# A four-layer gMLP, pooling and ConvFFN trunk on eight cores: tile-wise stage borders and a scheduler that orders all instructions, in place of hand-placed order

## The chip, the cores and the metric

One Trainium2 chip, all eight cores. Every core does one prompt sequence (2048 tokens) and 64 sample tokens, without talking to the others, so the work is the same on all. The time is the device time of the slowest core, in microseconds (us).

Some executions of the kernels here fell in a second, slower state: the cores of one die, or of both, show a lower granted TensorE clock, and the run is some per cent longer. All comparisons below are between runs outside that state ("fast" runs).

## The reference

Four layers. Even layers mix tokens by spatial gating in chunks of 128, odd ones by trailing means over 2, 4, 8 and 16 tokens. A gated feed-forward stage with a causal convolution of width 3 follows each. There is an RMS norm before every part.

```python
D_MODEL = 1024; SEQ = 2048; DEPTH = 4; CHUNK = 128; D_V = 2048; D_FF = 2816
def rmsnorm(x, g):
    y = x * lax.rsqrt(jnp.mean(x * x, axis=-1, keepdims=True) + EPS)
    return y * g
def gmlp_mixer(h, w_in, g_v, w_s, b_s, w_out):
    z = jax.nn.gelu(jnp.einsum('btd,de->bte', h, w_in))
    u, v = jnp.split(z, 2, axis=-1)
    v = rmsnorm(v, g_v)
    s = jnp.einsum('hij,bcjhe->bcihe', tril(w_s), chunks(v)) + b_s    # (names shortened)
    return jnp.einsum('bte,ed->btd', u * s, w_out), v
def pool_mixer(h, buf, start_pos, w_pool, scale): ...  # (mean - h) @ w_pool per group, x scale
def conv_ffn(h, buf, w_gate, w_val, conv_w, conv_b, w_down):
    a, val = h @ w_gate, h @ w_val
    conv = conv_b + conv_w[0]*a[t-2] + conv_w[1]*a[t-1] + conv_w[2]*a[t]
    return (jax.nn.silu(conv) * val) @ w_down
# trunk: x = x + mixer(rmsnorm(x)); x = x + conv_ffn(rmsnorm(x)); last: rmsnorm(x)
```

## The kernel before

The residual x lies transposed on the chip: 1024 channels as eight rows of 128 partitions, tokens along the columns. Two groups of 1056 tokens (1024 of the prompt and 32 sample tokens) are computed one after the other, each in three tiles of 352 columns. Weights stream through a ring of four slots.

An instruction is issued at once, in the order in which the code calls it, on an engine and with PSUM banks that the code names:

```python
PE.op(mmg, reads=ug["res"] + hr, writes=[bank_r[gbk]])   # op() puts the waits in front and issues
ACC_BANKS = [3, 4]; SSQ_BANKS = [0, 1, 2]; gbanks = [0, 1, 2]; vbanks = [5, 6, 7]
```

The projections at the end of a stage go by weights first: for each of the eight output rows all three token tiles. So all three tiles are complete only at the very end, together, and the last statistics, root and norm stand behind them:

```python
    def chunk(self, dc, mm_emit, evac_emit, hooks=None):
        last = (dc == KC - 1)
        for tt in range(3):
            ...
            mm_emit(dc, tt, bk)
            if self.pend is not None and tt == 0:
                norm_mm(self.pend)                 # statistics of row dc-1, on TensorE
            evac_emit(dc, tt, bk)                  # x += psum, on VectorE
            if last:
                norm_square(dc, tt)
                if tt >= 1: norm_mm(dc, tt - 1); norm_rstd(tt - 1)
        if last:
            norm_mm(dc, 2); norm_rstd(2)
            if keep_warm: ...                      # off (0)
```

In a gating stage ScalarE has Gelu, then a root, then Gelu again for each chunk of 128 tokens, with a load of its function table each way (ACT_TABLE_LOAD, 68 in the gating stages, 1283 ns each):

```python
ACT.op(... out=junk, in_=vsb, func=AF.Square, accum_out=vstat[:, 0:1])
ACT.op(... out=vstat[:, 1:2], in_=vstat[:, 0:1], func=AF.Sqrt, bias=epsb, scale=1.0 / DV)
DVE.op(... reciprocal(out=vstat[:, 2:3], in_=vstat[:, 1:2]))
DVE.op(... scalar_tensor_tensor(out=vb, in0=vsb, scalar=vstat[:, 2:3], in1=gvb, op0=mult, op1=mult))
```

In the feed-forward stage the gate is copied to SBUF (`asb`) so that two earlier columns can be read across tile borders; the first tap comes from PSUM on ScalarE, the other two from the copy on VectorE. x is loaded by rows of tokens and transposed on TensorE (fp32, 128 tokens at a time), and y goes back the same way.

Of the kernel before, what the change touches and what calls it, by code (L numbers as in the profile page):

```python
# [7 lines left out]
BF16 = mybir.dt.bfloat16  # L8
AF = mybir.ActivationFunctionType
# [11 lines left out]
NS = 32  # L21
NT = NP + NS
TT = 352
# [4 lines left out]
SLOT = 4096  # L28
NSLOT = 4
# [14 lines left out]
class Tick:  # L44
    __slots__ = ("sem", "val", "clock")

    def __init__(self, sem, val, clock):
        self.sem, self.val, self.clock = sem, val, clock
# [5 lines left out]

class Eng:
    def __init__(self, name, handle, sem, self_safe=False):
        self.name, self.h, self.sem, self.self_safe = name, handle, sem, self_safe
        self.count = 0
        self.know = {}
        self.nwaits = 0  # L60
        self.nops = 0

    def _wait(self, t):
        key = t.sem.name
        if self.know.get(key, 0) >= t.val:
            return
        self.h.wait_ge(t.sem, t.val)
        self.nwaits += 1
        self.know[key] = t.val
        for k, v in t.clock.items():  # L70
            if self.know.get(k, 0) < v:
                self.know[k] = v

    def op(self, fn, reads=(), writes=(), dsem=None):
        best = {}

        def add(t, raw):
            k = t.sem.name
            if k not in best:
                best[k] = [t, raw]  # L80
            else:
                if best[k][0].val < t.val:
                    best[k][0] = t
                best[k][1] = best[k][1] or raw
        for r in reads:
            for o in r.overl:
                if o.last_write is not None:
                    add(o.last_write, True)
                if r.space == "ps":
                    for t in o.reads:  # L90
                        add(t, False)
        for w in writes:
            for o in w.overl:
                if o.last_write is not None:
                    add(o.last_write, False)
                for t in o.reads:
                    add(t, False)
        for t, raw in best.values():
            if t.sem is self.sem and (self.self_safe or not raw):
                continue  # L100
            self._wait(t)
        ins = fn(self.h)
        self.nops += 1
        if dsem is not None:
            dsem.count += 16
            ins.then_inc(dsem.sem, 16)
            tick = Tick(dsem.sem, dsem.count, dict(self.know))
        else:
            self.count += 1
            ins.then_inc(self.sem, 1)  # L110
            tick = Tick(self.sem, self.count, dict(self.know))
        for r in reads:
            r.reads.append(tick)
            if len(r.reads) > 48:
                b = {}
                for t in r.reads:
                    k = t.sem.name
                    if k not in b or b[k].val < t.val:
                        b[k] = t
                r.reads = list(b.values())  # L120
        for w in writes:
            w.last_write = tick
            w.reads = []
        return tick

def tiles_of(c0, c1):
    return list(range(c0 // TT, (c1 - 1) // TT + 1))

def build_program(cfg=None):
    cfg = cfg or {}  # L130
    nlayers = cfg.get("nlayers", DEPTH)
    do_mixer = cfg.get("do_mixer", True)
    do_ffn = cfg.get("do_ffn", True)
    ngroups = cfg.get("ngroups", NG)
    layers = cfg.get("layers", list(range(nlayers)))
    pool_dbg = cfg.get("pool_dbg", 99)
    keep_warm = cfg.get("keep_warm", 0)

    nc = bass.Bass("TRN2", target_bir_lowering=False)
    dr = {}  # L140

    def din(name, shape):
        dr[name] = nc.dram_tensor(name, list(shape), F32, kind="ExternalInput").ap()
        return dr[name]

    def dout(name, shape):
        dr[name] = nc.dram_tensor(name, list(shape), F32, kind="ExternalOutput").ap()
        return dr[name]

    x_prompt = din("x_prompt", [SEQ, D])  # L150
    x_sample = din("x_sample", [NSEQ * 4, D])
    state_pool = din("state_pool", [2, NSEQ * 15, D])
    state_ffn = din("state_ffn_conv", [DEPTH, NSEQ * 2, DFF])
    norm_mix = din("norm_mix", [DEPTH, D])
    norm_ffn = din("norm_ffn", [DEPTH, D])
    norm_final = din("norm_final", [1, D])
    w_in_a = din("w_in_a", [2, D, 2 * DV])
    g_v_a = din("g_v_a", [2, DV])
    w_s_a = din("w_s_a", [2, 8, 128, 128])
    b_s_a = din("b_s_a", [2, 8 * 128])  # L160
    w_out_a = din("w_out_a", [2, DV, D])
    w_pool_b = din("w_pool_b", [2, 1024, 256])
    scale_b = din("scale_b", [2, D])
    w_gate = din("w_gate", [DEPTH, D, DFF])
    w_val = din("w_val", [DEPTH, D, DFF])
    conv_w = din("conv_w", [DEPTH * 3, DFF])
    conv_b = din("conv_b", [DEPTH, DFF])
    w_down = din("w_down", [DEPTH, DFF, D])
    c_ident = din("c_ident", [128, 128])
    c_maskT = din("c_maskT", [128, 128])  # L170
    c_icnt = din("c_icnt", [128, 64])

    y_prompt = dout("y_prompt", [SEQ, D])
    y_sample = dout("y_sample", [NSEQ * 4, D])
    gmlp_v = dout("gmlp_v_sample", [2, NSEQ * 4, DV])
    pool_prompt = dout("pool_prompt", [2, 15, D])
    pool_sample = dout("pool_sample", [2, NSEQ * 15, D])
    conv_prompt = dout("ffn_conv_prompt", [DEPTH, 2, DFF])
    conv_sample = dout("ffn_conv_sample", [DEPTH, NSEQ * 2, DFF])

    es = ExitStack()
    with es:
        ARENA_BYTES = 212800
        arena = es.enter_context(nc.sbuf_tensor("arena", [128, ARENA_BYTES // 4], F32))
# [4 lines left out]
        def al(x):  # L189
            return (x + 31) // 32 * 32  # L190

        def esz(dt):
            return 4 if dt == F32 else 2
# [4 lines left out]
        def alloc_at(name, shape, dt, off):  # L198
            nb = int(np.prod(shape[1:])) * esz(dt)
            assert off + nb <= base + ARENA_BYTES, (name, off + nb - base, ARENA_BYTES)  # L200
            return nc.alloc_sbuf_tensor_at(name, list(shape), dt, offset=off), nb

        def alloc(name, shape, dt, off=None, pieces=None):
            b = Buf()
            if off is None:
                off = cursor[0]
                adv = True
            else:
                adv = False
            b.t, nb = alloc_at(name, shape, dt, off)  # L210
            b.off = off
            b.nb = nb
            if adv:
                cursor[0] = off + (nb + 31) // 32 * 32
            b.r = {}
            if pieces is None:
                b.r[None] = Res(reg, "sb", off, off + nb, name)
                b.all = [b.r[None]]
            else:
                for key, lo, hi in pieces:  # L220
                    b.r[key] = Res(reg, "sb", off + lo * esz(dt), off + hi * esz(dt), f"{name}{key}")
                b.all = list(b.r.values())
            return b

        def grid_pieces(nrow, rowlen, ncols=NT, coloff=0):
            ps = []
            for k in range(nrow):
                for tt in range(3):
                    ps.append(((k, tt), k * rowlen + coloff + tt * TT, k * rowlen + coloff + (tt + 1) * TT))
            return ps  # L230

        xT = alloc("xT", [128, KC, NT], F32, pieces=grid_pieces(KC, NT))
        ring = [alloc(f"ring{i}", [128, SLOT], BF16) for i in range(NSLOT)]
        ident = alloc("ident", [128, 128], F32)
        maskT = alloc("maskT", [128, 128], F32)
        icnt = alloc("icnt", [128, 4, 16], F32)
        onesb = alloc("onesb", [128, 128], BF16)
        epsb = alloc("epsb", [128, 1], F32)
        pvd = alloc("pvd", [128, KC, 12], F32)
        pvf = alloc("pvf", [128, FC, 16], F32)  # L240
        wsT = alloc("wsT", [128, 2, 8, 128], BF16)
        msm = alloc("msm", [32, 2, 8, 32], BF16)
        brow = alloc("brow", [1, 2, 8, 32], BF16)
        brow.all = [Res(reg, "virt", i, i + 1, f"brow{i}") for i in range(16)]
        browM = alloc("browM", [1, EC, 128], BF16)
        browM.all = [Res(reg, "virt", 50 + i, 51 + i, f"browM{i}") for i in range(2)]
        msm.all = [Res(reg, "virt", 100 + i, 101 + i, f"msm{i}") for i in range(16)]
# [105 lines left out]
        def evac_copy(out_ap, in_ap, reads, writes, eng=None):  # L353
            evac_flip[0] ^= 1
            if eng is not None:
                evac_flip[0] = eng
# [819 lines left out]
```

## Time and profile before

| | |
|---|---|
| median | 3419.86 us (16 runs, 3413.87 to 3906.85) |
| fast runs | 3412 to 3428 us |
| TensorE busy | 3019.6 us of a span of 3416.6 (88%) |
| mean granted clock | 0.943 to 0.947 |
| columns streamed through TensorE | 6,654,520 in 19,338 matmuls |

The prediction shows the lines of this profile. In them PE is TensorE (matmuls), PEld its weight loads, DVE is VectorE, ACT ScalarE, POOL GpSimd and SP SyncE; psum is PSUM, which every matmul row of the profiles writes, and the other names are tiles in SBUF. The clock is the share of TensorE's full clock that the records show as granted. A row of slices has 40 digits, each the busy tenths of one fortieth of the span. A group of instructions reads: line, engine, operation, out<-in, shapes, count | busy us, mean ns | idle time of the engine in front of them, with what ended most of it. A timeline row reads: start, length, line, shapes, count, and in brackets the idle time before it and what ended it.

### The profile page before, as it was taken

How to read it: one execution, taken by the hardware profiler on the slowest of the kernel's cores; microseconds unless marked ns; L12 is line 12 of the kernel's file. 1: busy time of each engine (PE TensorE's matmuls, PEld its weight loads, DVE VectorE, ACT ScalarE, POOL GpSimd, SP SyncE). 2: the span in 40 equal slices, each digit the busy share in tenths (PEclk: the TensorE clock that was granted, in tenths of full speed). 3: DMA queues.
4: the chain of work that ended last, by engine and by line, in shares of the span. 5: the costliest groups of instructions: out<-in, count | busy, mean ns of one | idle time of the engine just before them, and what ended most of it. 6: DMA issues, size and time to landing. Idle time of an engine off the chain costs nothing.

```text
span 3416.6 us, 52100 instructions; the slowest of 8 cores (3406.7 to 3416.6 us)
## 1 busy us (share of the span) xinstructions
PE 3019.6 (88%) x19338; PEld 1886.7 (55%) x19338; DVE 1639.2 (48%) x3353; ACT 1406.5 (41%) x2766; POOL 233.5 (7%) x245
## 2 busy tenths in 40 slices
PE   3888997699998999589969899968999989986997
PEld 2545665366554566356645456635665456653665
DVE  1143763675223573567341457456721437636753
ACT  2362542254254452345234536334523626522541
POOL 1000000001100001000100000100011000000010
PEclk9898998799999999799979999989999999998999
DMA  5713366156571347224857124732487233651463
GB/s 111 103 16 55 56 75 78 19 75 74 71 99 18 62 63 82 39 44 63 87 148 99 18 46 76 75 50 45 63 100 103 30 55 52 79 79 20 75 67 68
DMA packets 369235, 225.23 MB, mean 66 GB/s; under 512 B 189457, under 2 KB 362689, under 8 KB 368346
## 3 DMA queue, kind: packets, MB, share of 16 engines
q0 software_dynamic: 352320, 190.87, 43.6%
q1 hardware_dynamic: 16666, 31.03, 2.9%
q8 instruction: 157, 2.57, 0.3%
q14 instruction: 92, 0.75, 0.1%
HBM read 399.41 MB, written 13.32 MB: 121 GB/s over the span
## 4 chain that ended last, share of the span: by engine, by line
PE 72%; DVE 11%; ACT 8%; issue 5%; DMA 3%; SPq 0%; DVEq 0%; ACTq 0%
PE psum L1094 18%; PE psum L1002 17%; PE psum L996 17%; PE psum L783 7%; PE psum L693 7%; DVE hB L521 4%; DVE vn L725 2%; ACT vsb L714 2%; PE psum L502 2%; ACT junk L720 2%; PE psum L878 2%; DMA xstg<-x_prompt 1%; ACT sq L489 1%; DVE pA L930 1%; PE psum L708 1%
## 5 line engine op out<-in xcount | busy, mean ns | idle before, releaser
L996 PE MATMUL psum<-hB,ring 128*128 128x352 bf16 x4224 | 726.9, 316 | 36.8 <-DVE hB L521 34.6
L1002 PE MATMUL psum<-hB,ring 128*128 128x352 bf16 x4224 | 723.9, 315 | 8.9 <-DVE mT L1054 7.7
L1094 PE MATMUL psum<-mT,ring 128*128 128x352 bf16 x4224 | 643.0, 313 | 0.0
L996 PEld LDWEIGHTS psum<-hB,ring 128*128 128x128 bf16 x4224 | 415.4, 99 | 263.3 <-issue 41.8
L1002 PEld LDWEIGHTS psum<-hB,ring 128*128 128x128 bf16 x4224 | 414.0, 98 | 236.2 <-issue 17.1
L1094 PEld LDWEIGHTS psum<-mT,ring 128*128 128x128 bf16 x4224 | 412.7, 98 | 217.0 <-issue 1.3
L489 ACT ACTIVATE sq<-xT 128x1056 bf16<-128x1056 f32 x128 | 137.6, 1082 | 918.1 <-DVE xT L1100 520.4
L1016 ACT ACTIVATE asb<-psum 128x352 f32<-128x352 f32 x528 | 240.2, 455 | 532.9 <-PE psum L996 299.4
L1026 DVE SCALAR_TENSOR_TENSOR c2b<-asb,pvf,c0b 128x352 f32<-128x352 f32 x528 | 302.0, 572 | 241.1 <-ACT c0b L1022 239.0
L1100 DVE TENSOR_TENSOR xT<-psum,xT 128x352 f32<-128x352 f32 x192 | 100.8, 525 | 537.1 <-PE psum L1094 533.5
L1022 ACT ACTIVATE c0b<-psum,pvf 128x352 f32<-128x352 f32 x528 | 340.5, 645 | 0.0
L1029 DVE SCALAR_TENSOR_TENSOR c2b<-asb,pvf,c2b 128x352 f32<-128x352 f32 x528 | 302.7, 573 | 55.1
L1053 ACT ACTIVATE gb<-c2b 128x352 f32<-128x352 f32 x528 | 263.4, 499 | 35.6 <-DVE c2b L1029 18.4
L1054 DVE TENSOR_TENSOR mT<-gb,psum 128x352 bf16<-128x352 f32 x528 | 271.6, 514 | 9.5 <-ACT gb L1053 8.7
L693 PE MATMUL psum<-hB,ring 128*128 128x352 bf16 x1536 | 247.8, 326 | 29.2 <-DVE hB L521 29.2
L783 PE MATMUL psum<-UB,ring 128*128 128x352 bf16 x1536 | 253.1, 327 | 16.2 <-DVE UB L764 11.1
L708 PE MATMUL psum<-R,hB 128*128 128x512 bf16 (+1 forms) x1152 | 254.9, 380 | 9.3 <-ACT vsb L714 9.2
L693 PEld LDWEIGHTS psum<-hB,ring 128*128 128x128 bf16 x1536 | 154.6, 101 | 122.2 <-issue 35.2
L783 PEld LDWEIGHTS psum<-UB,ring 128*128 128x128 bf16 x1536 | 155.2, 102 | 105.3 <-issue 17.0
L708 PEld LDWEIGHTS psum<-R,hB 128*128 128x128 bf16 (+1 forms) x1152 | 111.0, 98 | 142.8 <-issue 14.4
L724 DVE RECIPROCAL vstat<-vstat 128x1 f32<-128x1 f32 (+1 forms) x36 | 5.8, 162 | 357.4 <-ACT vstat L722 357.4
L697 ACT ACTIVATE UB<-psum 128x352 bf16<-128x352 f32 x192 | 88.9, 463 | 158.0 <-PE psum L693 158.0
(114 smaller groups left out, 2162.7 us busy)
## 6 DMA issues: line engine op xcount, KB each, us to landing
ring<-w_down POOLq DMA_DIRECT2D x64, 704.0 KB, 8.9
ring<-w_gate POOLq DMA_DIRECT2D x40, 1024.0 KB, 9.7
ring<-w_val POOLq DMA_DIRECT2D x40, 1024.0 KB, 13.3
ring<-w_in_a POOLq DMA_DIRECT2D x16, 1024.0 KB, 9.9
ring<-w_out_a POOLq DMA_DIRECT2D x16, 1024.0 KB, 23.5
R<-w_in_a POOLq DMA_DIRECT2D x16, 1024.0 KB, 28.1
xstg<-x_prompt SPq DMA_DIRECT2D x16, 512.0 KB, 5.1
y_prompt<-stg SPq DMA_DIRECT2D x16, 512.0 KB, 3.2
```

Source lines behind the costliest of these rows:

```text
L693: i = e.matmul(bank(bk, 0, TT), lhsT=wv[:, kc, (ec % 4) * 128:(ec % 4 + 1) * 128], rhs=hB.t[:, kc, cs], start=(kc == 0), stop=(kc == KC - 1))
L708: i = e.matmul(psum[0:ntok, n * 512:(n + 1) * 512], lhsT=hB.t[:, kc, col0:col0 + ntok], rhs=R2.t[:, n, kc, :], start=(kc == 0), stop=(kc = ...
L783: i = e.matmul(bank(bk, 0, TT), lhsT=wv[:, ec, (dc % 2) * 128:(dc % 2 + 1) * 128], rhs=UB.t[:, ec, cs], start=(ec == 0), stop=(ec == EC - 1))
L996: ins = e.matmul(bank(gbk, 0, TT), lhsT=ug["view"][:, kc, fo:fo + 128], rhs=hB.t[:, kc, cs], start=(kc == 0), stop=(kc == KC - 1))
L1002: ins = e.matmul(bank(vbk, 0, TT), lhsT=uv["view"][:, kc, fo:fo + 128], rhs=hB.t[:, kc, cs], start=(kc == 0), stop=(kc == KC - 1))
L1016: ACT.op(lambda e: e.activation(out=ab.t[:, 2 + pc0:2 + pc0 + npr], in_=bank(gbk, 0, npr), func=AF.Copy), reads=[bank_r[gbk]], writes=abw)
L1022: ACT.op(lambda e: e.activation(out=cb.t[:, :], in_=bank(gbk, 0, TT), func=AF.Identity, bias=pvf.t[:, fc, 12 + l:13 + l], scale=pvf.t[:, f ...
L1026: DVE.op(lambda e: e.scalar_tensor_tensor(out=c2.t[:, 0:npr], in0=ab.t[:, 1 + pc0:1 + pc0 + npr], scalar=pvf.t[:, fc, 3 * l + 1:3 * l + 2] ...
L1029: DVE.op(lambda e: e.scalar_tensor_tensor(out=c2.t[:, 0:npr], in0=ab.t[:, pc0:pc0 + npr], scalar=pvf.t[:, fc, 3 * l:3 * l + 1], in1=c2.t[: ...
L1053: ACT.op(lambda e: e.activation(out=gg.t[:, :], in_=c2.t[:, :], func=AF.Silu), reads=c2.all, writes=gg.all)
L1054: DVE.op(lambda e: e.tensor_tensor(out=mT.t[:, fc, cs], in0=gg.t[:, :], in1=bank(vbk, 0, TT), op=ALU.mult), reads=gg.all + [bank_r[vbk]], ...
L1094: i = e.matmul(bank(bk, 0, TT), lhsT=wv[:, fc, :], rhs=mT.t[:, fc, cs], start=(fc == 0), stop=(fc == FC - 1))
```

## The change

The intent is to keep TensorE fed across the borders of stages. The network stays the same. Nearly the whole program is rewritten; the parts that bear on the time:

```diff
 # 1. record everything, then put it in order
-    def op(self, fn, reads=(), writes=(), dsem=None):    # issues at once
+class Recorder:
+    def rec(self, eng, fn, reads=(), writes=(), cost=0.0, dsem=None, nbytes=0, tab=None, pt=()): ...
+    def schedule(self, engines, window=160):
+        # list scheduler: of the next 160 recorded operations of each engine, the one that can
+        # start first by modelled costs; a PSUM tile gets the banks that come free first
 ...
 # 2. token tiles: sizes, sample tokens all in the first group
-TT = 352
+TILES = {0: [(0, 384), (384, 384), (768, 320)], 1: [(0, 384), (384, 384), (768, 256)]}
 ...
 # 3. projections go tile by tile; what follows a tile is recorded right behind it
+            for t in range(3):
+                proj_tile(g, t, mm_list)
+                after_tile(t)      # statistics, root, norm; pooling; store y and load the next x
 ...
 # 4. statistics: squares added on GpSimd, one matmul closes the sum
-                        norm_mm(self.pend)
+            eng = POOL if kc < KC - 1 else DVE
+            rec(eng, lambda e: e.tensor_tensor(out=d.t[:, 0:n], in0=a.t[:, 0:n], in1=s.t[:, 0:n], op=ALU.add), ...)
 ...
 # 5. reciprocal root of the gating norm: seven tiny VectorE operations, no table change
-                        ACT.op(lambda e: e.activation(... func=AF.Sqrt ...))
-                        DVE.op(lambda e: e.reciprocal(...))
+                rsqrt_col(vs, nt)
 ...
 # 6. feed-forward: no copy; the gate is computed with two more columns, all taps read PSUM
-                        ACT.op(lambda e: e.activation(out=ab.t[:, 2 + pc0:2 + pc0 + npr], in_=bank(gbk, 0, npr), func=AF.Copy), ...)
+                                i = e.matmul(pap(gb, 0, n + 2), lhsT=wg.t[:, kc, fs], rhs=hB.t[:, kc, c0:c0 + n + 2], ...)
 ...
 # 7. pooling: product with w_pool first, then a banded matrix, placed between the tiles around it
+                            lst.append(((oc, oc + 128), zt.t[:, zh, es_], band.t[:, gi, :], True))
+                            lst.append(((oc, oc + 16), zp.t[:, zh, es_], bprev.t[:, gi, :], False))
 ...
 # 8. the host packs x, weights and state as they lie on the chip
-                PE.op(trx, reads=[sres] + ident.all, writes=[bank_r[bk]])        # transposes of x and y
+        m["x_in"] = np.concatenate(parts)
```

## The prediction

> **What bounds the kernel now.** I read the cores first: spans of 3406.7 to 3416.6 us and clocks of 0.943 to 0.947, both dies alike, so the profile fell in an undisturbed run. Then the busy table and the slices, the windows of the slices, the timeline of TensorE at the start and in two stages, the waits, and the groups by form.
>
> From the page of the kernel before:
>
> ```profile
> span 3416.6 us, 52100 instructions; the slowest of 8 cores (3406.7 to 3416.6 us)
> PE 3019.6 (88%) x19338; PEld 1886.7 (55%) x19338; DVE 1639.2 (48%) x3353; ACT 1406.5 (41%) x2766; POOL 233.5 (7%) x245
> ...
> PE   3888997699998999589969899968999989986997
> ...
> PEclk9898998799999999799979999989999999998999
> ...
> PE 72%; DVE 11%; ACT 8%; issue 5%; DMA 3%; SPq 0%; DVEq 0%; ACTq 0%
> ```
>
> TensorE is the bound (88% busy, 72% of the chain that ended last), no other engine is half full, and where the PE row dips (5, 6, 7) the clock row dips too. The same seen in windows of one slice each (PE busy, PEld, DVE, ACT, POOL, clock, DMA share, GB/s):
>
> ```profile
> 0.00:85.00 85.00, 27.77 (x134) 19.86 (x134) 8.59 (x21) 17.38 (x24) 13.35 (x29) 0.92 0.59 111
> 598.00:683.00 85.00, 55.17 (x318) 32.97 (x319) 52.89 (x99) 21.96 (x40) 0.96 (x1) 0.78 0.11 19
> 683.00:769.00 86.00, 86.00 (x578) 56.15 (x577) 62.59 (x157) 50.55 (x120) 5.24 (x6) 1.00 0.50 74
> 1708.00:1793.00 85.00, 58.07 (x322) 38.51 (x321) 38.27 (x71) 31.49 (x48) 2.78 (x4) 0.76 0.56 149
> ```
>
> In the feed-forward stage (683 to 769) TensorE never stops, is granted the whole clock, and does a 352-column matmul every 86.00/578 = 149 ns: 352/2.4 = 146.7 plus about 2.4 ns. At the start, in the pooling layer (598 to 683) and between the two token groups (1708 to 1793) it stands still a third to two thirds of the time, and its clock falls. So I split the span: columns streamed, 6,654,520 (counted in the built program) / 2.4 per ns = 2773; 19338 matmuls x 2.4 ns = 46; the 288 fp32 transposes take 1.94 us per eight instead of 0.43, so about 50 more: 2870 us if warm and never waiting. Busy is 3020, so 150 us are the slow clock. Idle is 3417 - 3020 = 397 us. What can be had by keeping TensorE fed is therefore up to about 550 us, and the rest is columns.
>
> Where the idle time is, from the timeline of TensorE (start, length, line; idle before it in brackets) at the first layer and in a gating stage:
>
> ```profile
> 97.05 2.50 PE L693 MATMUL psum<-hB,ring 128*128 128x352 bf16 x8 [5.11 <-DVE hB L521]
> ...
> 1888.42 1.02 PE L742 MATMUL psum<-browM,onesb 1*128 1x512 bf16 x4 [0.33 <-DVE vn L725]
> 1889.38 1.07 PE L745 MATMUL psum<-wsT,vn 128*128 128x128 bf16 x16
> 1890.82 7.07 PE L708 MATMUL psum<-R,hB 128*128 128x512 bf16 x32 [0.38 <-ACT vsb L714]
> ```
>
> The first layer matmul starts at 97 us: everything before is loading, transposing and normalising. A gating chunk costs 9.8 us with 0.7 us of waits. The groups that matter for the change:
>
> ```profile
> L1016 ACT ACTIVATE asb<-psum 128x352 f32<-128x352 f32 x352 | 163.4, 464 | 410.4 <-DVE asb L1012 233.3 <-PE psum L996 177.1
> L1022 ACT ACTIVATE c0b<-psum,pvf 128x352 f32<-128x352 f32 x528 | 340.5, 645 | 0.0
> L1029 DVE SCALAR_TENSOR_TENSOR c2b<-asb,pvf,c2b 128x352 f32<-128x352 f32 x352 | 205.6, 584 | 36.8
> L502 PE MATMUL psum<-sq,onesb 128*128 128x352 bf16 x432 | 102.5, 339 | 46.2 <-ACT sq L489 24.2 <-ACT sq L493 22.0
> L722 ACT ACT_TABLE_LOAD x36 | 46.2, 1283 | 3.0 <-ACT junk L720 0.4
> L714 ACT ACT_TABLE_LOAD x32 | 41.1, 1283 | 89.8 <-DVE vn L725 89.8
> ```
>
> [...] 0.78 and 0.76 in the broken windows, 1.00 in the dense one. [...] in 690 to 840 and 2395 to 2555 us all eight cores have TensorE 99% busy, at 1.00. [...] 1283 ns[...], 68 times in the gating stages. [...]
>
> **The change part by part.** It is a rewrite of the same network: all arrays are packed on the host in the layout that is used on the chip, and all instructions are first recorded and then put in order by a list scheduler that gives PSUM banks as they come free.
>
> 1. Columns of TensorE. The big products stay (gate, value, down, u, out: 352 columns on average, the gate with two halo columns, +8,448 columns). Gone: 288 x and y transposes and most of 432 statistics matmuls, now 180, since squares are added on GpSimd and one matmul closes the sum (-89,000 columns); the sample tokens form one chunk instead of two (64 v matmuls, -33,000). Pooling becomes product first, then a banded matrix of 128 or 16 columns: 181,376 columns become 117,504. The built program has 18,552 matmuls with 6,423,424 columns: 2676 + 18,552 x 2.4 ns = 45, plus some 10 us for band matmuls that are too short to stream at this rate: 2731 us. Against 2870 that is -139.
> 2. Start. x arrives transposed, in tiles of 384 tokens, and tile 0 goes first. Half a tile is 0.79 MB; 0.5 MB took 5.1 us, so about 10 us for both; squares, statistics, Ln/Exp with a table load and eight normalisations of 575 ns: the first layer matmul at about 20 us, not 97. Then the weights: a unit of 1 MB landed in 9.9 us; eight are needed for u and v, about 80 us, against some 60 us of u work, so another 18 us of waiting: about 38 us idle, where before it was about 70 idle and 27 of transposes.
> 3. Group change. Loading, storing and the first norm go tile by tile behind the last down product (176 matmuls of 162 ns, 28 us per tile) and the next u product (128, 21 us per tile): from about 27 us idle before (window 1708) to near 0.
> 4. Gating. The reciprocal root moves from Sqrt on ScalarE plus reciprocal to seven tiny VectorE operations: 68 table loads x 1283 = 87 us of ScalarE are gone, and the 0.7 us wait per chunk shrinks. The chain per chunk is Square 1.9 + accumulator read 0.2 + seven x about 0.2 + scaling 2.35 + two Gelus 2.0 = 7.9 us, below the 8.9 of TensorE. I allow 0.2 x 34 = 7 us.
> 5. Pooling. It is put between the tiles of the down product before it and the feed-forward stage after it. VectorE there: per tile eight evacuations of 582 and eight norms of 575 = 9.3 us, twice after the last down tile, plus another norm and the state: some 25 us in about 40 us in which the feed-forward itself needs 27. So 8 us may show in each of four pooling layers: 32, against about 60 in each now (stall plus slow clock).
> 6. Feed-forward. The copy to asb goes (240 us of ScalarE); the taps read PSUM. VectorE stays at 0.58 + 0.58 + 0.51 = 1.67 us of 2.39 us per step, ScalarE falls to 0.65 + 0.5. TensorE was full and stays full: no gain of time, but slack for the norms.
> 7. The other twelve borders of stages: the next stage begins on tile 0 while tile 2 is normalised; 2 us each, 24. End: statistics 3, Ln/Exp 2.4, eight norms 4, store 4: 15 us.
>
> Sum: 2731 + 38 + 7 + 32 + 24 + 15 = 2847. I take 2845.
>
> **The rivals.** (a) Clock. [...] For: one of four runs of before took 3557. Against: the dense windows at 1.00 on all cores. I give it a tenth[...]. (b) GpSimd. It has to issue the weights and now also adds 216 squares and four small operations for each of 88 sample steps, in order; a weight load that waits for its slot holds the adds behind it. [...] (c) Drift: the order is fixed with modelled costs, and where real durations differ an in-order engine waits for the wrong one. Each per cent is 27 us. (d) Weights: 382 MB are read as before, now 16 KB in one piece; at the 9.9 us per unit seen they fill 20 of 28.6 us of a gate/value unit. As the bound it would show as PE waits for DMA; I expect that only at the start. (e) The scheduler is better than I allow at the pooling layers: 2790.
>
> **Range and chances.** Centre 2845, a ratio of 0.83. (e) gives the low side, (b) and (c) together the high side, and half of (a) lies outside. 2770 to 2960. Even all of (b) and (c) leaves it far below 3350, so only (a) could make it not faster: faster 0.96, same 0.03, slower 0.01.
>
> **What would show it.** TensorE busy 95% or more of the span, near 2740 to 2760 us, mean clock above 0.97, no slice below 9 but the first and last; the first u matmul near 20 us; no Sqrt table loads; VectorE near 55% and ScalarE near 45%; the pooling matmuls spread over the down stage without stalls of 5 us. I am wrong if the clock is below 0.95 in dense windows, if GpSimd is named in long waits of TensorE's suppliers, or if dips remain at the eight layer borders.

The 0.78, 0.76 and 1.00 are the granted clocks of its windows, and 1283 ns is one table load. The pace behind the 2731, 2.4 columns per ns and 2.4 ns for each matmul, agrees with the profiles where the clock is 1.00: 149 ns per matmul at 352 columns (kernel before), 109.1 at 256 and 162.6 at 384 (88 in 9.60 us and 74 in 12.03, from the last third of the changed kernel's first profile). There a band matmul of 128 columns and one of 16 together take 81 ns, where this pace would give 65; the 10 us for such matmuls are an estimate.

## The result, and the profile after

| | before | after |
|---|---|---|
| median of all runs | 3419.86 us (16 runs) | 2847.16 us (11 runs, 2845.59 to 3036.28) |
| ratio of fast runs | | 0.8329, 95% interval 0.832 to 0.8338 |
| TensorE busy | 3019.6 us (88%) | 2749.4 us (97%) |
| TensorE idle | 397 us | 95 us |
| mean granted clock | 0.943 to 0.947 | 0.990 to 0.991 |

A ratio is the mean time of one kernel's fast runs over that of the other's fast runs of the same rounds, so it is not quite the ratio of the medians. The result is correct.

The first profile of the changed kernel fell in the slow state. From its page:

```profile
span 3166.1 us, 51168 instructions; the slowest of 8 cores (3139.8 to 3166.1 us)
...
PEclk8788888788888888887888788899999999999999
```

TensorE is as full there as one could wish, yet the span is 320 us longer, and the clock row rises from 7 and 8 to 9 for the last third. Such a page must not be read for the change. So the unchanged kernel was run again, and its page shows the fast state:

```profile
span 2844.5 us, 51201 instructions; the slowest of 8 cores (2843.7 to 2844.5 us)
PE 2749.4 (97%) x18552; PEld 1747.5 (61%) x18552; DVE 1475.6 (52%) x2798; ACT 1155.0 (41%) x2179; POOL 470.1 (17%) x832
...
PE   5999999999999999999999999999999999999998
...
PEclk9999999999999999999999999999999999999999
...
PE 87%; DVE 6%; ACT 4%; issue 2%; DMA 1%; DVEq 0%; ACTq 0%; SPq 0%
```

The dips of the PE row are gone but for the first and last slice, and the clock row has none left. The chain that ended last is 87% TensorE instead of 72%. Windows of one slice (PE busy, PEld, DVE, ACT, POOL, clock, DMA share, GB/s) at the start, in a pooling layer and at the end:

```profile
0.00:71.00 71.00, 39.17 (x191) 20.66 (x192) 19.61 (x42) 25.51 (x44) 11.44 (x25) 0.93 0.98 193
...
498.00:569.00 71.00, 66.29 (x507) 44.05 (x506) 48.74 (x99) 41.75 (x69) 9.42 (x17) 0.98 0.46 86
...
2773.00:2844.00 71.00, 60.18 (x428) 41.56 (x426) 23.18 (x47) 13.67 (x27) 13.34 (x16) 0.95 0.18 60
```

In the pooling window TensorE stands still for 71 - 66.29 = 4.7 us; the pooling window shown of before had 29.8. In the first 71 us 31.8 are idle, in the last 71 us 10.8.

What happens at a border, from the timeline of TensorE (from the gating layer's last projection into the feed-forward stage):

```profile
236.39 15.37 PE L701 MATMUL psum<-UB,w 128*128 128x320 bf16 x112
251.60 1.47 PE L937 MATMUL psum<-hB,w 128*128 128x386 bf16 x8
...
254.21 0.30 PE L652 MATMUL psum<-accb,meanb 128*128 128x320 bf16 x1
```

The feed-forward matmul (L937) starts in the same breath as the projection (L701) ends. It works on tile 0, which was normalised while tile 2 was still being projected. The statistics of tile 2 (L652) are closed only two groups later. In the kernel before, the same border has 1.58 + 3.40 us of standing still (the rows are shown with the run that fills them, below).

### The profile page after: what moved, and what is told of

Same layout as the page of the kernel before. It is cut to its first block, busy times and chain, and to the rows that moved or that the text cites. A ratio compares the mean times of both kernels' runs of the same rounds, so it can differ in the third digit from the quotient of the medians.

```text
span 3166.1 us, 51168 instructions; the slowest of 8 cores (3139.8 to 3166.1 us)
## 1 busy us (share of the span) xinstructions
PE 3087.4 (98%) x18519; PEld 1868.6 (59%) x18552; DVE 1482.4 (47%) x2798; ACT 1165.1 (37%) x2179; POOL 470.1 (15%) x832
## 3 DMA queue, kind: packets, MB, share of 16 engines
q8 instruction: 153, 2.51, 0.3%
## 4 chain that ended last, share of the span: by engine, by line
PE 93%; DVE 3%; ACT 2%; issue 1%; DMA 1%; DVEq 0%; SPq 0%; ACTq 0%
PE psum L701 30%; PE psum L937 22%; PE psum L944 22%; PE psum L749 8%; PE psum L769 7%; PE psum L851 1%; DVE hB L664 1%; PE psum L796 1%; PE psum L641 1%; DVE vn L779 1%; DMA xT<-x_in 1%; ACT junk L776 1%; ACT vsb L774 0%; PE psum L898 0%; PE psum L793 0%
## 5 line engine op out<-in xcount | busy, mean ns | idle before, releaser
L937 PE MATMUL psum<-hB,w 128*128 128x386 bf16 (+2 forms) x4224 | 802.9, 338 | 0.0
L944 PE MATMUL psum<-hB,w 128*128 128x384 bf16 (+2 forms) x4224 | 797.1, 336 | 0.0
L961 DVE SCALAR_TENSOR_TENSOR cb<-psum,pvf,cb 128x384 f32<-128x384 f32 (+1 forms) x1056 | 597.4, 571 | 297.1 <-ACT cb L951 203.4
L701 PE MATMUL psum<-mT,w 128*128 128x384 bf16 (+2 forms) x4224 | 704.9, 334 | 0.0
L937 PEld LDWEIGHTS psum<-hB,w 128*128 128x128 bf16 x4224 | 438.6, 104 | 272.6 <-issue 3.0
L944 PEld LDWEIGHTS psum<-hB,w 128*128 128x128 bf16 x4224 | 437.6, 104 | 270.1 <-issue 1.7
L701 PEld LDWEIGHTS psum<-mT,w 128*128 128x128 bf16 x4224 | 436.2, 103 | 262.6
L951 ACT ACTIVATE cb<-psum,pvf 128x384 f32<-128x384 f32 (+2 forms) x528 | 338.6, 642 | 490.5 <-PE psum L937 488.5
L974 DVE TENSOR_TENSOR mT<-cb,psum 128x384 bf16<-128x384 f32 (+2 forms) x528 | 271.7, 517 | 256.4 <-ACT cb L973 220.7
L749 PE MATMUL psum<-hB,w 128*128 128x384 bf16 (+2 forms) x1536 | 272.5, 347 | 9.9 <-DVE hB L664 9.9
L769 PE MATMUL psum<-w,hB 128*128 128x512 bf16 (+1 forms) x1055 | 277.3, 425 | 4.6 <-ACT vsb L774 1.9
L701 PE MATMUL psum<-UB,w 128*128 128x384 bf16 (+2 forms) x1536 | 268.7, 344 | 0.0
L749 PEld LDWEIGHTS psum<-hB,w 128*128 128x128 bf16 x1536 | 163.5, 107 | 116.8 <-issue 17.6
L701 PEld LDWEIGHTS psum<-UB,w 128*128 128x128 bf16 x1536 | 162.3, 106 | 101.8
```

The costliest lines, as they stand in the source:

```text
L701: ins = e.matmul(pap(bk, 0, n), lhsT=lt, rhs=rh, start=(i == 0), stop=(i == len(mms) - 1))
L749: i = e.matmul(pap(bk, 0, n), lhsT=ub.t[:, kc, e4 * 128:(e4 + 1) * 128], rhs=hB.t[:, kc, 2 + c0:2 + c0 + n], start=(kc == 0), stop=(kc == ...
L769: i = e.matmul(pap(bks, q * 512, (q + 1) * 512)[0:nt, :], lhsT=hB.t[:, kc, 2 + col0:2 + col0 + nt], rhs=w.t[:, kc, :], start=(kc == 0), st ...
L937: i = e.matmul(pap(gb, 0, n + 2), lhsT=wg.t[:, kc, fs], rhs=hB.t[:, kc, c0:c0 + n + 2], start=(kc == 0), stop=(kc == KC - 1))
L944: i = e.matmul(pap(vb, 0, n), lhsT=wv.t[:, kc, fs], rhs=hB.t[:, kc, 2 + c0:2 + c0 + n], start=(kc == 0), stop=(kc == KC - 1))
L951: rec(ACT, lambda e: e.activation(out=cb.t[:, 0:n], in_=pap(gb, 2, 2 + n), func=AF.Identity, bias=sc(12 + l), scale=sc(3 * l + 2)), pt=[(g ...
```

## The experiments

Twelve runs were made: the changed kernel once more, eight variants of it, and three of the kernel before. In the diffs, lines are cut to what differs.

### The changed kernel once more

No edit.

> The changed kernel once more, unaltered, because its first profile fell in the slow state (clock held at 0.81 until about 2080 us). Theory (TensorE is fed without a gap, and its columns set the time): in a fast run about 2847 us, TensorE busy near 2745 us, some 100 us idle, of which about 45 at the start and the end, and a mean clock of 0.99. Rival [...]: clock of 0.81 to 0.9 in dense windows of fast runs too.

Measured: fast runs 2845.4 to 2848.8 us, ratio 0.8324 (0.8294 to 0.8354); the profile above. The result repeats, and the busy time, 2749.4 us, is 18 us above the prediction's floor of 2731. By the clock records of this trace TensorE is busy for 47 us at half clock (the first 34 us, before the first record, counted by the pace of the matmuls), which costs some 24 us; in the kernel before it was 244 us (223 by the records, the rest by the pace before the first record), some 122 lost. So the clock takes little in this kernel, where TensorE is busy for 97% of the span.

### What order alone is worth

First a window of 1: every engine runs its operations in the order in which they were recorded.

```diff
-        order = R.schedule(engines)
+        order = R.schedule(engines, window=1)
```

> The changed kernel with every engine taking its instructions in the recorded order (window of the list scheduler 1 instead of 160). Theory A (the tile-by-tile structure and the column count make the gain, the scheduler adds what the gating chunks need): in the recorded order the spatial product of a chunk follows its own v product at once, so 34 chunks wait for Gelu 1.0, Square 2.1, seven tiny operations 1.2 and scaling 2.35, some 6.7 us each: +230 us; the pooling tiles in the down stage add some 40 to 80 of stall and slow clock: about 3120 to 3200. Rival B (order matters little, the engines' queues absorb it): below 2900. Rival C (the scheduler is all of the gain): 3400 or more.

Measured: one fast run, 4846.98 us, the others 4881 to 5095. Only rival C covers that ("3400 or more"), and no theory had the reason, mine included. The waits of TensorE in its profile (slow state, so only their kind and rough size count; columns: what waits, for what, us in total, times, longest):

```profile
PE psum L701 <- DMA w<-wts: 613.1, 64, 12.8
...
PE psum L793 <- DVE vn L779: 249.3, 32, 7.9
```

The wait for VectorE's `vn` is the one I had expected (I had said 230). But weights dominate: over all lines of the list they make some 1050 us, because a weight load is recorded only where it is first used. The scheduler has been doing the prefetch too, which my expectation overlooked. So the second run leaves GpSimd and SyncE, which issue the transfers, free:

```diff
-            while i < L and n < window:
+            win = window if name in ("pool", "sp") else 1
+            while i < L and n < win:
```

> The recorded order again for TensorE, ScalarE and VectorE, but GpSimd and SyncE may be reordered by the scheduler, so that weights are fetched ahead; in the run with all engines in recorded order TensorE waited about 1040 us for weights, since a load was issued where it was first used. Theory (prefetch was the larger half of the loss, the gating chain and the pooling tiles the rest): 3500 to 3750, TensorE waiting about 250 us for the scaled v and no more than 100 for weights. Rival (the order on the compute engines is what costs): 4300 or more.

Measured: one fast run, 3696.92 us, as expected; the profile was taken in it. TensorE is busy for 3014.7 us (82%).

```profile
PE psum L794 <- DVE vn L780: 249.6, 32, 8.1
PE psum L642 <- ACT sqb L614: 212.8, 108, 14.9
```

The weights are gone from the list but for one wait of 5.0 us. What is left is one wait per gating chunk (32 times 7.8 us) and the statistics. So of the scheduler's gain, by fast runs, 4847 - 3697 = 1150 us is the prefetch of weights and 3697 - 2847 = 850 us the order of computing. Each rests on one fast run of either kernel, so these are sizes, not exact. They are not a share of the gain over the kernel before: that one had its own, hand-made prefetch and interleaving. The rewrite gave those up and needs the scheduler to have them back.

### Tile-by-tile borders taken away

The norms behind a projection wait until the last row of tile 2 is done, as in the kernel before. What the changed kernel records behind a tile (pooling, and at the change of group the load and first norm of the next tile) moves behind all three tiles with them; the rest stays.

```diff
+            for t in range(3):
+                border[0] = [xT.r[(KC - 1, 2)]]      # the norms read this too
                 after_tile(t)
+                border[0] = []
```

> The changed kernel in which the norms after a projection wait until all three tiles have been projected, so that the next stage can't begin on tile 0 while tile 2 is still being projected. Theory (tile-wise borders hide the norm): after each of 14 projections followed by a norm TensorE waits for a statistics matmul, Ln and Exp with a table load 2.4, eight norms of 575 ns 4.6, about 7.5 us, plus some 3 us at half clock, in all 10 x 14 = +140 us: 2960 to 3010. Rival (the borders are filled by other work, or the border is short): below 2890.

Measured: 3026.1, 3026.2 and 3045.3 us in fast runs, but the result was wrong (relative error 0.053). Two buffers held the sum of squares, `accb[t % 2]`, and with the tiles moved together tile 2 wrote over tile 0 before it was used. The time can't be taken as it stands, since the shared buffer may have added waits of its own. Mended with a third buffer:

```diff
+        accb.append(alloc("accb2", [128, 384], BF16, off=X0 + 14784))
-            ab = accb[t % 2]
+            ab = accb[t]
```

> The run in which norms wait for all three tiles, repaired: the bf16 sums of squares have three buffers, where tile 2 overwrote tile 0's before, which made the values wrong. Same work, so the same time as that run on its undisturbed cores: about 3024 us (+180), TensorE idle about 235 us and 40 us more busy by the slow clock. If the wrong buffer had added waits of its own, it falls to 2960 to 3010, the range of the first expectation.

Measured: correct. The ratio of fast runs is 0.8886 (0.8848 to 0.8924), but in each of them some cores have a lower clock than the others; the fastest took 3022.41 us. In the profiled run six cores have spans of 2987.0 to 2996.3 us at a clock of 0.967 to 0.972, and two have 3040 and 3044 at 0.951 and 0.950. By the undisturbed six the cost is 143 to 152 us over 2844. That is below what I expected of the mended run; it falls in the range 2960 to 3010 that was given for the first one. The border shown above, on an undisturbed core:

```profile
254.71 0.30 PE L653 MATMUL psum<-accb,meanb 128*128 128x320 bf16 x1 [3.75 <-DVE accb L631]
258.42 2.73 PE L943 MATMUL psum<-hB,w 128*128 128x386 bf16 x8 [3.41 <-DVE hB L667]
```

Two waits, for the sum and for the norm, and a first group at half pace: 2.73 us instead of 1.47. So in this kernel going tile by tile is worth about 150 us, a quarter of the size of the whole gain. The edit touches twelve borders (four behind a gating stage, eight behind a feed-forward stage), so some 12 us each on average; the two waits and the half pace shown here make 8.4 of that, at this one. On this core TensorE is idle for 114 us more and busy for 28 us more than in the changed kernel. The wait for the sum comes twelve times, 44 us in all; the four pooling layers have 71 us idle instead of 26, and the change of group some 18 more, so the 150 us are the price of the order there too, and not of twelve equal borders.

### The slow clock behind a wait, filled

A switch of the kernel before puts idle matmuls behind the last statistics of a stage. If the low clock behind a border were the loss, this would give it back.

```diff
-    keep_warm = cfg.get("keep_warm", 0)
+    keep_warm = cfg.get("keep_warm", 20)
```

> The kernel before, with 20 idle matmuls put behind the last statistics matmul of every projection stage, so that TensorE is busy while VectorE normalises. Theory: the low mean clock of the kernel before is a consequence of its waits; behind a border wait of 3.40 us the next layer matmuls take 2.51, 2.55 and 1.76 us per eight instead of 1.36, so about 2.7 us are lost after each such border. The filler lasts some 3 us and should restore 1.36 from the first group. Ten of the sixteen borders have a wait of this length (the four before a pooling layer wait 16 us and are not filled, the two at the end of a token group neither), so about 25 us less: 3390 to 3400, the waits as long as before. Rival: the clock has another cause[...], the groups behind a border stay near 2.5 us, and the time stays at 3410 to 3425, or rises by up to 40 us because the filler stands in front of real work.

Measured: ratio to the kernel before 1.0042 (1.0026 to 1.0058), so about 14 us slower. The border in the kernel before, and in this one:

```profile
325.44 0.31 PE L502 MATMUL psum<-sq,onesb 128*128 128x352 bf16 x1 [1.58 <-ACT sq L493]
329.15 2.51 PE L996 MATMUL psum<-hB,ring 128*128 128x352 bf16 x8 [3.40 <-DVE hB L521]
331.45 2.55 PE L1002 MATMUL psum<-hB,ring 128*128 128x352 bf16 x8
...
339.47 1.36 PE L996 MATMUL psum<-hB,ring 128*128 128x352 bf16 x8
```

```profile
323.64 0.31 PE L502 MATMUL psum<-sq,onesb 128*128 128x352 bf16 x1 [1.57 <-ACT sq L493]
323.79 3.14 PE L566 MATMUL psum<-sq,onesb 128*128 128x352 bf16 x20
327.36 1.35 PE L996 MATMUL psum<-hB,ring 128*128 128x352 bf16 x8 [0.43 <-DVE hB L521]
...
331.33 1.35 PE L996 MATMUL psum<-hB,ring 128*128 128x352 bf16 x8 [1.42 <-DVE hB L521]
...
337.68 1.36 PE L996 MATMUL psum<-hB,ring 128*128 128x352 bf16 x8
```

VectorE's norms lie beside it, before and with the filler (lines of the same timelines):

```profile
324.95 11.99 DVE L521 SCALAR_TENSOR_TENSOR hB<-xT,pvd,rstd 128x352 bf16<-128x352 f32 x24 [0.24 <-ACT rstd L534]
```

```profile
323.16 11.99 DVE L521 SCALAR_TENSOR_TENSOR hB<-xT,pvd,rstd 128x352 bf16<-128x352 f32 x24 [0.26 <-ACT rstd L534]
```

The theory was right about the clock: with the filler the first group takes 1.35 us, not 2.51 (in the kernel before the clock is 0.50 from 329.15 to 331.40 us, and 1.00 from 336 on). It was wrong about the time. From the start of the last statistics matmul to the start of the fourth gate group (the last row of each fence) it is 339.47 - 325.44 = 14.03 us before and 337.68 - 323.64 = 14.04 us with the filler. The second and the third gate group now wait 1.42 us each for what the slower matmuls came too late to wait for: VectorE normalises for 11.99 us in both runs, and only then clears the buffer (`asb`) into which ScalarE empties the gate's PSUM. So VectorE sets the pace, and the slow clock behind this wait cost nothing. The 14 us are lost elsewhere. On core 3 of both profiles the time from the last pooling matmul to the first gate matmul grows by 3.0 us in each of the four pooling layers (7.5, 7.5, 9.1 and 9.0 us before, 10.5, 10.5, 12.0 and 12.0 with the filler). There the filler stands in front of the transposes of the pooling state (L959), for which VectorE waits before it normalises: 4.41 us instead of 1.44 in the first of them. The change of group and the end grow by some 2 us each.

### Two of the parts alone, in the kernel before

The reciprocal root on VectorE:

```diff
-ACT.op(... func=AF.Sqrt ...); DVE.op(... reciprocal ...)
+tiny(... add eps); tiny(... shift right); tiny(... 1597463007 - i); 2 x (tiny(...); tiny(...))
```

> The kernel before with one part of the change alone: the reciprocal root of the gating stages by seven tiny VectorE operations instead of Sqrt with its table loads and a reciprocal. Theory (step 4): the chain of a chunk falls from about 9.8 to about 7.9 us, below TensorE's 9.1, so the wait of 0.7 us per chunk goes: -23 us, about 3397. Rival (the wait is only moved to VectorE): within 6 us of 3420.

Measured: fast runs 3394.0, 3394.4 and 3410.3 us, ratio 0.995 (0.9904 to 0.9996); some 22 us less than the fast runs of the same rounds (3414 to 3420) by the two lower ones, about what I expected.

x and y packed on the host, no transposes of them:

```diff
-        def load_x_tr(g, c): ... e.transpose(...)
+        def load_x(g, tt):
+            SP.op(lambda e: e.dma_start(out=xT.t[:, ks, cs], in_=v[:, ks, cs]), ...)
```

> The kernel before with one part of the change alone: x comes transposed and y goes out transposed, so the 288 fp32 transposes with their copies and staging are gone; norms, order and stages stay whole. Theory (steps 2 and 3, and the end): about -27 us at the start (the set-up of the gating weights still stands before the first product), -45 at the change of group, -20 at the end: about 3325, 3300 to 3360. Rival (they overlap with transfers that have to be waited for anyway): 3400 or more.

Measured: two fast runs, 3395.4 and 3396.2 us (four slow ones up to 3848). Some 21 us less than the fast runs of the same rounds, where I had expected some 90; a miss. From the timeline of its start:

```profile
83.68 1.94 PE L465 MATMUL psum<-ident,stg 128*128 128x128 f32 x8 [11.17 <-DMA stg<-w_s_a]
90.72 2.50 PE L651 MATMUL psum<-hB,ring 128*128 128x352 bf16 x8 [5.10 <-DVE hB L519]
```

The first layer matmul comes at 90.72 instead of 97.05 us. The set-up transposes of the gating weights and their transfers, which wait for 11.17 us at a time, still stand in front of it in program order. At the group change nothing is won: from the last statistics of the first group to the first matmul of the second it is 52.7 us in both kernels (1717.17 to 1769.87, and 1725.92 to 1778.63), since the load of x has to wait for the final norm of all of it and TensorE now waits 37.8 us at a stretch for the squares. Only the end is shorter: from the last statistics matmul to the end of the span 16 us, not 32. The transposes had lain beside waits; removing them without moving the order lets the waits show.

These two parts together make some 43 of the 572 us.

### Parts taken back in the changed kernel

Statistics of the projections on TensorE:

```diff
-                stat_add(g, t, dc)
+                stat_add_pe(g, t, dc)
```

> The changed kernel with the statistics of the projections summed by TensorE again (eight matmuls per tile instead of one after GpSimd adds): 252 more matmuls of 352 columns. Theory (every column of TensorE is on the path): 252 x 149 ns = +37.5 us, so about 2884, less at most 5 because the chain through GpSimd at the end is shorter. Rival (the statistics were hidden in gaps, or the GpSimd chain cost as much): within 10 us of 2847.

Measured: the three fast runs took 2895 to 2922 us, partly on one disturbed die; cores of the other die 2891 to 2894 against 2844, so 48 us more, 10 above what I expected; some 42.5 of it are busy time of TensorE (2792 on such a core). The 252 more matmuls (18,804 instead of 18,552) cost what their columns cost, 37.5 us, and a little more. So moving the sums to GpSimd is worth 48 us: GpSimd, 470 us busy with them and 266 without, gives back nothing measurable of what TensorE saves.

Sqrt on ScalarE again:

```diff
-                rsqrt_col(vs, nt)
+                rec(ACT, ... func=AF.Sqrt, ... tab="sqrt"); rec(DVE, ... reciprocal ...)
```

> The changed kernel with Sqrt on ScalarE and one reciprocal on VectorE in the gating stages, as in the kernel before, in place of the seven tiny operations. Theory (step 4): the chain of a chunk grows by two table loads 2.56, Sqrt 0.3 and reciprocal 0.16, less 1.2 for the tiny operations, from 7.9 to 9.7 us, above TensorE's 8.9: +0.8 x 34 = +27 us, about 2874. Rival (other TensorE work fills the wait, since the scheduler may put u or out products between): within 8 us of 2847.

Measured: fast runs 2867.4 to 2868.2 us, so 21 us more, where I had expected 27. In its groups:

```profile
L769 PE MATMUL psum<-w,hB 128*128 128x512 bf16 x993 | 226.2, 383 | 16.8 <-ACT vsb L774 15.0 <-issue 0.2
```

Of the table loads 64 are back (34 for the root, 30 for the Gelu after it, 1283 ns each), 82 us of ScalarE. TensorE's wait for the Gelu of the v product rises from 6.2 to 15.0 us in all, and its busy time by 6.5 us; so a quarter of the ScalarE time reaches the end. The same part in the kernel before was worth about the same, 22 us.

The gate copied to SBUF (bf16), the taps from there:

```diff
+                        gc = gcp[step[0] % 2]
+                        rec(ACT, ... out=gc.t[:, 0:npr + 2], in_=pap(gb, 0, npr + 2), func=AF.Copy ...)
-                            in0=pap(gb, 2 - sh, 2 - sh + npr)
+                            in0=gc.t[:, 2 - sh:2 - sh + npr]
```

> The changed kernel with the gate copied to SBUF by ScalarE again (528 copies of about 455 ns, +240 us of ScalarE) and the taps read from there. Theory (step 6: TensorE was full in the feed-forward stage and stays full, so the removed copy bought no time): 2842 to 2855. Rival (the longer chain and ScalarE at about 50% delay PSUM banks or the norms): 2870 or more.

Measured: 2856.3 to 2857.6 us, ratio 0.8355; 9 us more, just above what I expected. ScalarE is busy for 1338 us instead of 1155, so 183 us of ScalarE bring 9 us of time. The taps themselves, changed kernel first:

```profile
L961 DVE SCALAR_TENSOR_TENSOR cb<-psum,pvf,cb 128x384 f32<-128x384 f32 x704 | 429.1, 616 | 140.9 <-ACT cb L951 114.6 <-ACT cb L973 1.1 <-ACT sqb L613 1.0
```

```profile
L965 DVE SCALAR_TENSOR_TENSOR cb<-gcp,pvf,cb 128x384 f32<-128x384 bf16 x704 | 430.0, 619 | 69.1 <-ACT gcp L962 36.9 <-DVE cb L965 1.4 <-issue 0.4
```

616 ns from PSUM, 619 from SBUF in bf16: VectorE does not mind where it reads here. The gain of leaving out the copy is ScalarE's alone.

### A better start

In the changed kernel the first weights and constants share the transfers with the first x tile (DMA share 0.98 in the first slice). Here the x tiles go first, each after the one before it, the first weights are released as x lands, and the constants that are needed later are held until x is there.

```diff
-            load_x(0, t)
+            load_x(0, t, [xT.r[(7, t - 1)]])
+            unit(("Uu", 0, 0, t))
+            late = [xT.r[(7, 2)]]
-            const_load(band, ...)
+            const_load(band, ..., hold=late)
```

> The changed kernel with another order of its first transfers only: x tile 0 alone first, then the first u weights; x tile 1 waits for tile 0, tile 2 for tile 1, the second u weights for x tile 0, the third and fourth for x tile 1, and constants, the pool state copy and the v weights for x tile 2. In the fast profile the second half of x tile 0 landed at 17.8 us and the first u matmul ran at 28.7, not at 20 as I had predicted, because the transfer shares the engines (DMA share 0.98 in the first 71 us). Theory: the first u matmul moves to about 20 us and the u product, 58 us of work, ends at about 88 instead of 104: 2830 to 2840 in all. Rival (the start is bound by the bytes, 13 MB, whatever their order): 2844 to 2850.

Measured: fast runs 2834.1 to 2836.3 us, ratio 0.8292 (0.8276 to 0.8308), as expected. The timeline of the start and of the first product of the spatial weights (`brow`, then `wsT`), in the changed kernel and here:

```profile
18.48 1.12 PE L641 MATMUL psum<-sqb,meanb 128*128 128x384 bf16 x3 [6.55 <-ACT sqb L613]
...
28.73 2.72 PE L749 MATMUL psum<-hB,w 128*128 128x384 bf16 x8 [3.30 <-DVE hB L664]
...
135.41 0.39 PE L793 MATMUL psum<-brow,onesb 1*128 1x512 bf16 x4
```

```profile
11.94 2.09 PE L644 MATMUL psum<-sqb,meanb 128*128 128x384 bf16 x5 [0.17 <-DVE sqb L619]
25.66 12.80 PE L752 MATMUL psum<-hB,w 128*128 128x384 bf16 x64 [11.62 <-DMA w<-wts]
...
115.64 0.40 PE L796 MATMUL psum<-brow,onesb 1*128 1x512 bf16 x4 [0.88 <-DVE vn L782]
```

The second half of the statistics no longer waits 6.55 us for the second half of x. Now the first layer matmul waits for its weights instead, but then runs 64 in a row. So the number came as expected, but not by the path: the first u matmul moved to 25.66 and not to 20, and the v product begins at 100.78 us instead of 103.76 (I had said 88), so the start gives only 3 us. The other 10 come in the first gating stage. The scheduler, given other transfers, chose another order there: the first spatial product runs at 115.64 us, after the v products of two chunks, and not at 135.41, after those of four, and between 71 and 213 us TensorE is idle for 3.3 us instead of 10.7. The feed-forward stage begins at 238.12 us instead of 251.60. This is the fastest version that was run.

## Why the prediction was right, and where its steps were off

It said 2845 us in 2770 to 2960, faster; the median is 2847.16. The main step held: TensorE is the bound, columns are the floor, and nearly all idle time and slow clock are gone. That the tile-wise borders alone do this is not shown: taken away, they cost about 150 us. The busy time came out at 2749 us (said: 2740 to 2760), the clock at 0.990 (said: over 0.97), no slice but the first and the last is below 9, VectorE is at 52% (said: near 55), ScalarE at 41 (near 45).

But the sum hit closer than its terms did; errors cancelled:

| term of the sum | predicted | measured |
|---|---|---|
| busy time of TensorE | 2731 us | 2749 |
| start, idle | 38 | 32 |
| gating and group change, idle | 7 + 0 | about 20 + 6 (windows with gating stages; window 1493 to 1564) |
| pooling, idle | 32 | about 26 |
| other borders, idle | 24 | about 0 |
| end, idle | 15 | 10.8 |

- **Busy time.** 18 us over the floor; the half clock shown by the records, some 24 us, accounts for it within what such an estimate can say.
- **Start.** The first layer matmul was to come near 20 us and came at 28.73. The step "half a tile in about 10 us for both" failed: the squares of the second half are waited for until 18.48, because the first weights share the transfers. The total of the idle time was near all the same, because the weights after it were less of a hindrance than I took: that is luck. With x first the second half no longer waits, but then the weights do, and the start as a whole gains 3 us.
- **Gating.** The step "chain of 7.9 us, below the 8.9 of TensorE, 7 us in all" was too low. The waits of TensorE for `vn` (10.0 us), for the Gelu (6.2) and the short ones beside them add up to more. The reason for the size of each wait was not tested.
- **Borders.** Two us for each of twelve were given; the timeline shows none. That they would cost if tiles finished together is shown: about 150 us.
- **Feed-forward.** "No gain of time" from leaving out the copy: it is 9 us. Small, but not nothing.
- **The 550 us to be had.** I split before into 397 us idle and 150 us of slow clock, and called the sum what feeding TensorE could bring. 302 us of idle time did go. The other part was misread: 1.94 us for eight transposes is the pace at half clock (at 90.00 us, clock 0.50), and eight such back to back take 1.06 us at full clock (at 1753.60 us, in the change of group, clock 1.00). So the warm floor of the kernel before is about 2843 and not 2870, the remainder 177 and not 150, and the fall of the floor 112 and not 139; the 2847 does not rest on this. Nor is the remainder all slow clock: by the clock records, and the pace before the first of them, some 122 us were lost to it before and 24 after, so some 98 went. The filler shows that idle time and clock are not independent: at the border looked at, the clock could be had without any time coming back. I take it that it went here because VectorE was taken off the path; no run shows this apart.
- **Where the idle time went.** Between the last down product and the first gate product of the four pooling layers TensorE stood still for 167 us in the kernel before, and the windows of these layers now have 26. That is 141 of the 302 us, the largest share; the start gave some 35 and the change of group some 18. With the borders held together the pooling layers have 71 us, so tile-wise borders are 45 of the 141. The rest belongs to the new form of pooling, its placement or the scheduler: no run takes the new pooling back alone, and this stays open.

**The rivals.** (a) A low clock in dense work in all runs: no. The fast profiles of both kernels have 1.00 in dense windows, and the changed kernel's eight cores a mean of 0.990 to 0.991. The slow profile of the changed kernel has 0.81 to 0.82 until about 2080 us and 0.99 to 1.00 after it, with TensorE busy for 99% (520 to 2080 us) and 97% of the time; what starts and ends that these runs do not show. (b) GpSimd: its additions took 740 ns at 256 columns, 862 at 320 and 1000 at 384, but they lie beside other work; in the lists of what ScalarE and VectorE wait for, the largest entry with GpSimd is 34 us, in small pieces. (c) Drift from modelled costs: no run tested it alone; the model has such an addition at 1.13 us, and the run with a better start shows that another order of one gating stage is worth some 10 us. (d) Weights: no wait of TensorE for them is in the list of the changed kernel; at the start they share the transfers with x. (e) Pooling better than allowed: by 6 us, not 55.

## What to carry to other kernels

Before a slow clock or a removed instruction is priced, find who sets the pace behind it: a filler that restored the full clock, and transposes taken from a start, brought nothing or a quarter of the expected because VectorE or a transfer was the bound there. Of the parts that were taken back, order was worth most, about 150 us against 48, 21 and 9 for the others: let a stage finish its tiles one after the other, so that the norm of the first is done while the last is still computed, and let the next stage begin there. If a list scheduler makes the order, remember that it may also be making your prefetch, and when you test it by taking it away, free the engines that issue transfers first.
